# The dense tokens' second layers as three products of hi and lo parts, with nine row buffers in place of twelve

## The chip, the cores and the metric

The kernel runs on one core of a Trainium2 chip. The metric is the device time of one execution in microseconds; less is better. Rows of the profile name the engines: PE is TensorE (PEld its weight loads), DVE VectorE, ACT ScalarE, POOL GpSimd and SP SyncE.

## The reference, cut to what matters

Two transformer blocks run one after the other. The last layer of the second is a retrieval of single-neuron experts (`peer_ffn`), for 512 tokens of width 1024 with 16,384 experts. Each token has eight heads with 16 chosen experts each:

```python
idx = jnp.take_along_axis(cand_i, top_pos, axis=-1)
gate = jax.nn.softmax(top_s.astype(jnp.float32), axis=-1).astype(h.dtype)
...
act = jax.nn.gelu(jnp.einsum('thkd,td->thk', expert_u[ib], hb), approximate=False)
return jnp.einsum('thk,thkd->td', gb * act, expert_v[ib])
```

The first layer is a dot product of a token with a row of `expert_u`, then a GELU and the gate; the second layer is the weighted sum of rows of `expert_v`. The result is added to `x` and normalized. All of it is float32.

## The kernel before

The retrieval (`phase_d`) treats its 512 tokens in two ways. The first 256 (NS = 2 blocks of 128) are gathered: for every token and choice one row of `peer_u_rows` is fetched by an indirect DMA from GpSimd (128 rows of 4 KB each, 0.524 MB a gather, 128 gathers a block), and VectorE makes the dot product (L1355). Later the rows of `peer_v` are fetched the same way, and TensorE sums them: four gathers make a group, and a group is multiplied in one burst of eight float32 matmuls with a 32-column weight (L1384). The other 256 tokens (ND) are dense: all 16,384 experts are computed for them in NJ = 128 steps of 128 experts, and the gate, which is zero nearly everywhere, is multiplied in.

The last stage of the kernel is the loop over these 128 steps. A step has a weight `w` of 128 experts by 256 tokens (in SBUF as `ge` for the first 68 steps, and loaded back as `gl` and multiplied with the gate, loaded as `g`, on VectorE for the last 60, in groups of four steps: L1474, L1476, L1481), and a half of `vp`, a load of 128 x 2 x 1024 float32 (1 MB) of `peer_v` made once in two steps on SP's queue from a ring of four buffers. It multiplies them in four matmuls of 128x128 by 512 (L1495), two for each block of 128 tokens. The profile shows each of these float32 matmuls as two records.

The same loop advances two generators. `gathered_u` yields once for each gathered `peer_u` row and is pulled once a step in the first 60 steps, as long as rows are left; 50 of the 256 are. `gathered_v` is pulled every second step: it fetches the four gathers of the group two ahead, and then issues the burst of the group that is due. Both take their buffers from `gather`, which holds a list `rp` of two pools, `sb` with six row buffers and `lp` with six, and takes them strictly in turn. TensorE's instructions of the loop keep the order of the program; those of the other engines are ordered by the framework's scheduler when the kernel is built. Each engine then works in that fixed order, and waits for semaphores.

`x` is the dense tokens' input to the first layer, in `sb`, [128, 8, 256]; it has no reader once the first layers are done. Elsewhere in the kernel hi and lo parts are used already: `split` (L59, L60) makes a hi part with a ScalarE copy into a float32r tile, and a lo part by a VectorE subtraction, and `mm3` (L71) makes three products of them.

Of the kernel before, what the change touches and what calls it, by code (L numbers as in the profile page):

```python
# [11 lines left out]
FT = mybir.dt.float32  # L12
FR = mybir.dt.float32r
# [5 lines left out]
AF = mybir.ActivationFunctionType  # L19
OP = mybir.AluOpType  # L20
# [3 lines left out]
D = 1024  # L24
# [1091 lines left out]
def phase_d(k):  # L1116
    tc, nc, I = k.tc, k.nc, k.I
    gain = lambda n, c: k.vecs[:, VOFF[n] + c:VOFF[n] + c + 1]
    tt, ts, stt = nc.vector.tensor_tensor, nc.vector.tensor_scalar, nc.vector.scalar_tensor_tensor
    act = nc.scalar.activation  # L1120
    hx = k.hT[:, :, NM:]

    NJ, JG, TB, ND, NS = 128, 4, 32, 256, 2
# [7 lines left out]
    with ExitStack() as ctx:  # L1131
        dr = ctx.enter_context(tc.tile_pool(name="d_dram", bufs=1, space=bass.MemoryType.DRAM))
        sb = ctx.enter_context(tc.tile_pool(name="d_sb", bufs=1, reuse_waits="tile"))
# [21 lines left out]
        x = sb.tile([128, 8, ND], FT, name="x")  # L1155
        ht = [sb.tile([128, D], FT, name=f"ht{j}") for j in range(NS)]
        for s in range(2):
            o = slice(N0 * s, N0 + ND * s)
            for c in range(8):
                y = x[:, c] if s else xs[c // 4][:, c % 4]  # L1160
# [171 lines left out]
        out, rp = {}, []  # L1332

        def residual(po, j):

            hr = lp.tile([128, 8, 128], FT, name="hr", bufs=1)
            nc.scalar.dma_start(hr, hdr[:, :, 128 * j:128 * j + 128])
            for c in range(8):
                nc.tensor.matmul(po[c // 4][:, 128 * (c % 4):128 * (c % 4) + 128], hr[:, c], k.ident,
                                 start=False, stop=False, skip_group_check=True)  # L1340
# [56 lines left out]
        def pull(g, n):  # L1397
            for _ in range(n):
                if next(g, 0) == 0:
                    return False  # L1400
            return True
# [29 lines left out]
        for n in range(JR + JP):  # L1431
# [4 lines left out]
            else:  # L1436
                i = (n - JR) % JG
# [13 lines left out]

        lp = ctx.enter_context(tc.tile_pool(name="d_lp", bufs=2, reuse_waits="tile"))
        ps = ctx.enter_context(tc.tile_pool(name="d_po", bufs=1, reuse_waits="tile", space=PS))
        rp.append((lp, 6))
        for j in range(NS, 4):
            out[j] = [ps.tile([128, 512], FT, name=f"o{j}{i}") for i in range(2)]
        z = lp.tile([128, 4096], FT, name="z", bufs=1)
# [7 lines left out]
        def ahead(i):  # L1465

            if i >= NJ or ns[i] < JR:
                return
            n, j = ns[i], ns[i] % JG
            if j == 0:  # L1470
                g = lp.tile([128, NG, JG, TB], FT, name="g4", bufs=2)
                w = lp.tile([128, JG, ND], FT, name="gl", bufs=2)
                gl[n // JG] = w, g
                nc.scalar.dma_start(g, gdr[:, :, n - JR:n - JR + JG].rearrange("b p j t -> p b j t"))  # L1474
                if n < JR + JP:
                    nc.scalar.dma_start(w, st[:, n - JR:n - JR + JG])  # L1476
            w, g = gl[n // JG]
            if n >= JR + JP:
                u_chunk(n, w[:, j])
            b = w[:, j].rearrange("p (b t) -> p b t", t=TB)  # L1480
            tt(b, b, g[:, :, j], op=OP.mult)  # L1481
# [3 lines left out]
        with tc.manual_schedule(engines={mybir.EngineType.PE}):  # L1485
            for i in range(AH):
                ahead(i)
            for i, n in enumerate(ns):
                ahead(i + AH)
                if i % 2 == 0:  # L1490
                    vp = k.load(I["peer_v"].rearrange("(a j) d -> a j d", j=NJ)[:, n:n + 2], [128, 2, 1024])
                w = gl[n // JG][0][:, n % JG] if n >= JR else ge[n // JA][:, n % JA]
                for t in range(ND // 128):
                    for c in range(2):
                        nc.tensor.matmul(out[NS + t][c], w[:, 128 * t:128 * t + 128],  # L1495
                                         vp[:, i % 2, 512 * c:512 * c + 512],
                                         start=i == 0, stop=i == NJ - 1, skip_group_check=True)
                    if i == 0:
                        residual(out[NS + t], NS + t)
                if i < NJ // 2 - 4:  # L1500
                    pull(ga, 1)
                if i % 2:
                    pull(rows_left, 1)
# [4 lines left out]
        for j in range(4):  # L1508
            y = sb.tile([128, D], FT, name="rows", bufs=6)
# [13 lines left out]
def body(ctx, tc, I, out):  # L1523
# [37 lines left out]
    phase_b(k)  # L1561
    phase_c(k)
    phase_d(k)


# [106 lines left out]
```

## Time and profile before

| | |
|---|---|
| median of 3 runs | 3019.58 us (3007.23 to 3020.39) |
| the profiled execution's own time | 3018.37 us |
| its span in the profile | 3016.6 us |
| TensorE busy in the span | 2713.6 us (90%) |
| VectorE, ScalarE, GpSimd busy | 1224.5, 623.2, 591.7 us |
| mean transfer rate over the span | 303 GB/s |

The loop that is changed runs from about 2389 us to the end. Busy time counts an engine's instructions, and the ends of matmuls are modelled, so a busy TensorE need not be at its peak. The DMA share is the mean busy share of the core's 16 DMA engines; packets that overlap can take it a little over 1. A gather is timed from its issue on GpSimd to the landing of its last byte.

### The profile page before, as it was taken

What the parts mean: (1) busy time and instruction counts of PE and PEld (TensorE: products, weight loads), DVE (VectorE), ACT (ScalarE), POOL (GpSimd) and SP (SyncE); (2) the same over time, 40 slices, a digit from 0 to 9 for tenths busy, and PEclk for the clock granted to TensorE, in tenths of its full rate; (3) what the DMA queues carried; (4) which work ended last, traced back from release to release, by engine and by line L of the source; (5) the groups of instructions that cost most, each with busy time, mean ns of one, the idle gap of its engine ahead of it and who ended that gap; (6) DMA issues with size and microseconds to landing.
All of it is one profiled execution on the core that took longest, in us unless ns stands there. A gap on an engine that the chain in (4) does not pass through costs nothing. (4 is left out here: it accounts for less than half of the span.)

```text
span 3016.6 us, 35266 instructions
## 1 busy us (share of the span) xinstructions
PE 2713.6 (90%) x13794; PEld 1594.1 (53%) x13794; DVE 1224.5 (41%) x3040; ACT 623.2 (21%) x1304; POOL 591.7 (20%) x600
## 2 busy tenths in 40 slices
PE   8999888887888777699999997999998499999997
PEld 6877422322232222377777786888887333333332
DVE  5444411111111111268855389985888522200001
ACT  4333200000000000265333121122555300000000
POOL 1000100000000000000000005454433256544442
PEclk9979999999999999899999998999999699999999
DMA  4104899999999999912113239999999699999996
GB/s 158 42 1 154 367 421 421 421 421 421 420 421 420 421 421 376 376 60 85 56 56 112 92 132 355 365 381 361 379 363 350 225 399 412 412 410 363 401 401 252
DMA packets 185453, 912.93 MB, mean 303 GB/s; under 512 B 18864, under 2 KB 38464, under 8 KB 112192
## 3 DMA queue, kind: packets, MB, share of 16 engines
q1 hardware_dynamic: 83664, 602.85, 49.7%
q0 software_dynamic: 73728, 268.47, 23.0%
q10 hardware_dynamic: 27888, 39.29, 3.6%
q8 instruction: 110, 1.80, 0.2%
q14 instruction: 63, 0.52, 0.0%
HBM read 890.61 MB, written 19.92 MB: 302 GB/s over the span
## 5 line engine op out<-in xcount | busy, mean ns | idle before, releaser
L1328 PE MATMUL pa<-x,w 128*128 128x256 f32 x2048 | 455.4, 381 | 0.0
L1328 PEld LDWEIGHTS pa<-x,w 128*128 128x128 f32 x2048 | 385.9, 191 | 50.6
L1355 DVE SCALAR_TENSOR_TENSOR rows<-rows,ht 128x1024 f32<-128x1024 f32 x256 | 310.5, 1218 | 237.5 <-DMA rows<-in_peer_u_rows,ia 211.4
L1346 POOL DMA_INDIRECT rows<-in_peer_u_rows,ia x256 | 287.8, 1124 | 440.1 <-DVE rows L1355 211.1
L1346 POOL DMA_INDIRECT rows<-in_peer_v,iat x256 | 253.0, 988 | 292.1 <-PE os L1384 151.1
L712 PE MATMUL pr<-w,xs 128*32 128x512 f32 x1024 | 212.4, 697 | 91.6 <-DMA w<-in_expert_up 91.4
L732 PE MATMUL px<-w,ht 128*32 128x512 f32 x1024 | 223.2, 599 | 44.9 <-DMA w<-in_expert_down 35.5
L1495 PE MATMUL o<-w,ge 128*128 128x512 f32 x544 | 243.4, 600 | 0.0
L1495 PE MATMUL o<-w,gl 128*128 128x512 f32 x480 | 215.5, 602 | 4.4 <-DVE gl L1481 4.4
L71 PE MATMUL pm<-xg,w8h 128*128 128x512 f32 x640 | 206.4, 402 | 3.5 <-ACT cc L942 1.4
L712 PE MATMUL pg<-w,xs 128*32 128x512 f32 x1024 | 178.7, 612 | 19.3 <-DMA w<-in_expert_gate 19.3
L960 POOL MEMSET acc<- 128x1024 f32 x1 | 1.0, 952 | 936.4 <-PE px L732 936.4
L712 PEld LDWEIGHTS pr<-w,xs 128*32 128x32 f32 x1024 | 46.0, 124 | 245.1 <-DMA w<-in_expert_up 168.7
L1495 PEld LDWEIGHTS o<-w,ge 128*128 128x128 f32 x544 | 100.8, 191 | 139.4 <-issue 139.4
L732 PEld LDWEIGHTS px<-w,ht 128*32 128x32 f32 x1024 | 53.4, 109 | 203.0 <-DMA w<-in_expert_down 95.8
L718 DVE SCALAR_TENSOR_TENSOR hd<-pr,ga,hd 128x512 f32<-128x512 f32 x16 | 12.0, 751 | 361.6 <-PE pr L712 361.6
L1495 PEld LDWEIGHTS o<-w,gl 128*128 128x128 f32 x480 | 89.4, 191 | 131.0 <-issue 122.9
L1384 PE MATMUL os<-rows,z 128*32 128x512 f32 x1024 | 144.6, 600 | 5.4 <-DMA rows<-in_peer_v,iat 4.3
L1481 DVE TENSOR_TENSOR gl<-gl,g 128x256 f32<-128x256 f32 x60 | 21.5, 420 | 305.2 <-DMA gl<-st 305.2
L71 PEld LDWEIGHTS pm<-xg,w8h 128*128 128x128 f32 x640 | 120.8, 190 | 33.7 <-ACT w8h L59 2.0
L745 DVE TENSOR_TENSOR hT<-hT,po 128x512 f32<-128x512 f32 x128 | 86.0, 687 | 128.7 <-PE po L744 127.3
L59 ACT ACTIVATE w8h<-w 128x1024 fp32r<-128x1024 f32 (+3 forms) x101 | 90.8, 901 | 218.7 <-PE pm L71 106.3
(561 smaller groups left out, 3601.8 us busy)
## 6 DMA issues: line engine op xcount, KB each, us to landing
w<-in_expert_up SPq DMA_DIRECT2D x128, 1024.0 KB, 19.8
w<-in_expert_gate SPq DMA_DIRECT2D x128, 1024.0 KB, 19.8
w<-in_expert_down SPq DMA_DIRECT2D x128, 1024.0 KB, 19.8
w<-in_peer_u SPq DMA_DIRECT2D x64, 1024.0 KB, 8.1
w<-in_peer_v SPq DMA_DIRECT2D x64, 1024.0 KB, 8.3
w<-in_peer_wq SPq DMA_DIRECT2D x16, 1024.0 KB, 4.8
w<-in_w_out SPq DMA_DIRECT2D x8, 1024.0 KB, 4.8
st<-kept ACTq DMA_DIRECT2D x15, 512.0 KB, 9.3
```

The lines of the kernel that those rows point to most:

```text
L59: nc.scalar.activation(hi, src, AF.Copy)
L71: nc.tensor.matmul(o, w[:, c, :], x[:, c, s], start=first and c == 0 and n == 0, stop=last and c == kc - 1 and n == 2)
L712: nc.tensor.matmul(p[s], xs[:, 4 * half + c, s], ws[e][:, c], start=half == 0 and c == 0, stop=half == 1 and c == 3, skip_group_check=True)
L718: stt(hd, pu, ga[:, 1:2], hd, op0=OP.mult, op1=OP.mult)
L732: nc.tensor.matmul(pd[n][s], ht[:, 2 * half + f, s], ws[e][:, f, 512 * n:512 * n + 512], start=half == 0 and f == 0, stop=half == 1 and f ...
L745: tt(hx[:, c], hx[:, c], p, op=OP.add)
L1328: nc.tensor.matmul(p[:, :ND], w[:, c], x[:, c], start=c == 0, stop=c == 7)
L1346: nc.gpsimd.indirect_dma_start(out=r, out_offset=None, in_=rows, in_offset=bass.IndirectOffsetOnAxis(ap=idx, axis=0))
L1355: stt(r, r, 1.0, ht[j], op0=OP.mult, op1=OP.mult, accum_out=dots[:, n:n + 1])
L1384: nc.tensor.matmul(po[i][32 * g:32 * g + 32], z[:, o:o + 32], rs[g][:, 512 * i:512 * i + 512], start=r == 0, stop=r == 31, skip_group_chec ...
L1481: tt(b, b, g[:, :, j], op=OP.mult)
L1495: nc.tensor.matmul(out[NS + t][c], w[:, 128 * t:128 * t + 128], vp[:, i % 2, 512 * c:512 * c + 512], start=i == 0, stop=i == NJ - 1, skip_ ...
```

## The change

The dense tokens' second layer, one float32 matmul for each pair of operands, becomes three matmuls of float32r parts: hi by hi, hi by lo, and lo by hi. For that, each step makes hi and lo parts of the weight (`wp`, two buffers) and of the half of `vp` (`vs` in `lp` for even steps, and the tile `x` in `sb` for odd ones, one buffer each), by copies on ScalarE (`act`) and subtractions on VectorE (`tt`). The room comes from the row buffers of `lp`, which are three now and not six; `sb` keeps six.

```diff
-        rp.append((lp, 6))
+        rp.append((lp, 3))
...
                 w = gl[n // JG][0][:, n % JG] if n >= JR else ge[n // JA][:, n % JA]
+
+                wp = lp.tile([128, 2, ND], FR, name="wp", bufs=2)
+                vs = (sb if i % 2 else lp).tile([128, 2, D], FR, name="x" if i % 2 else "vs", bufs=1)
+                for y, z2 in ((w, wp), (vp[:, i % 2], vs)):
+                    act(z2[:, 0], y, AF.Copy)
+                    tt(z2[:, 1], y, z2[:, 0].bitcast(FT), op=OP.subtract)
                 for t in range(ND // 128):
-                    for c in range(2):
-                        nc.tensor.matmul(out[NS + t][c], w[:, 128 * t:128 * t + 128],
-                                         vp[:, i % 2, 512 * c:512 * c + 512],
-                                         start=i == 0, stop=i == NJ - 1, skip_group_check=True)
+                    for m, (hw, hv) in enumerate(((0, 0), (0, 1), (1, 0))):
+                        for c in range(2):
+                            nc.tensor.matmul(out[NS + t][c], wp[:, hw, 128 * t:128 * t + 128],
+                                             vs[:, hv, 512 * c:512 * c + 512], start=i == 0 and m == 0,
+                                             stop=i == NJ - 1 and m == 2, skip_group_check=True)
```

## Rows read from the trace of the kernel before

**Rows 1.** The page: busy time, share of the span and instructions by engine.
```profile
PE 2713.6 (90%) x13794; PEld 1594.1 (53%) x13794; DVE 1224.5 (41%) x3040; ACT 623.2 (21%) x1304; POOL 591.7 (20%) x600
```

**Rows 2.** Windows of the last stage: busy by engine, clock, DMA share, GB/s.
```profile
core 0: us, PE busy (x) PEld busy (x) DVE busy (x) ACT busy (x) POOL busy (x), PEclk, DMA share, GB/s
...
2440.00:2665.00 225.00, 220.96 (x718) 77.90 (x716) 53.35 (x87) 0.31 (x1) 134.40 (x133) 1.00 1.02 412
...
2732.00:2980.00 248.00, 248.00 (x888) 94.14 (x888) 17.21 (x48) 0.00 (x0) 105.91 (x112) 1.00 1.02 396
```

**Rows 3.** TensorE's timeline, first part: start, us, group [idle before]; first, middle, last.
```profile
2405.74 1.92 PE L1384 MATMUL os<-rows,z 128*32 128x512 f32 x16 [0.55 <-ACT z L1378]
...
2564.21 7.13 PE L1495 MATMUL o<-w,ge 128*128 128x512 f32 x16
2571.28 1.06 PE L1384 MATMUL os<-rows,z 128*32 128x512 f32 x6
2572.54 1.90 PE L1384 MATMUL os<-rows,z 128*32 128x512 f32 x10 [0.20 <-DMA rows<-in_peer_v,iat]
2574.37 7.13 PE L1495 MATMUL o<-w,ge 128*128 128x512 f32 x16
...
2674.20 1.92 PE L1384 MATMUL os<-rows,z 128*32 128x512 f32 x16
```

**Rows 4.** TensorE's timeline, second part.
```profile
2855.08 1.92 PE L1384 MATMUL os<-rows,z 128*32 128x512 f32 x16
2856.93 7.13 PE L1495 MATMUL o<-w,gl 128*128 128x512 f32 x16
2864.00 1.92 PE L1384 MATMUL os<-rows,z 128*32 128x512 f32 x16
```

**Rows 5.** VectorE's timeline, second part.
```profile
2829.38 1.43 DVE L1481 TENSOR_TENSOR gl<-gl,g 128x256 f32<-128x256 f32 x4 [17.06 <-DMA gl<-st]
2847.93 1.43 DVE L1481 TENSOR_TENSOR gl<-gl,g 128x256 f32<-128x256 f32 x4 [17.12 <-DMA gl<-st]
```

**Rows 6.** TensorE's timeline in an earlier stage that uses hi and lo parts.
```profile
1449.24 0.63 PE L71 MATMUL pm<-xg,w8h 128*128 128x512 f32 x2
...
1451.35 0.63 PE L71 MATMUL pm<-xg,w8h 128*128 128x512 f32 x2
```

**Rows 7.** Groups by line and shape: the splits; busy us, mean ns, idle before.
```profile
L59 ACT ACTIVATE w8h<-w 128x1024 fp32r<-128x1024 f32 x71 | 74.9, 1056 | 140.1 <-PE pm L71 52.7 <-PE uu L71 23.4 <-issue 17.8
...
L59 ACT ACTIVATE w8h<-w 128x256 fp32r<-128x256 f32 x8 | 3.3, 412 | 9.5 <-PE uu L71 4.8 <-PE mm L71 4.7
...
L60 DVE TENSOR_TENSOR w8l<-w,w8h 128x1024 fp32r<-128x1024 f32 x71 | 87.6, 1235 | 35.6 <-ACT w8h L59 34.9
...
L60 DVE TENSOR_TENSOR w8l<-w,w8h 128x256 fp32r<-128x256 f32 x8 | 3.4, 419 | 1.5 <-ACT w8h L59 1.5
```

**Rows 8.** GpSimd's timeline, second part.
```profile
2848.34 1.17 POOL L1346 DMA_INDIRECT rows<-in_peer_v,iat  x1 [4.25 <-PE os L1384]
2849.81 0.94 POOL L1346 DMA_INDIRECT rows<-in_peer_v,iat  x1 [0.30 <-issue]
2851.06 0.94 POOL L1346 DMA_INDIRECT rows<-in_peer_v,iat  x1 [0.30 <-issue]
```

**Rows 9.** GpSimd's timeline, first part.
```profile
2564.37 1.37 POOL L1346 DMA_INDIRECT rows<-in_peer_v,iat  x1 [0.34 <-PE os L1384]
...
2570.70 0.94 POOL L1346 DMA_INDIRECT rows<-in_peer_v,iat  x1 [1.28 <-DMA rows<-in_peer_v,iat]
...
2574.54 1.37 POOL L1346 DMA_INDIRECT rows<-in_peer_v,iat  x1 [0.34 <-PE os L1384]
```

**Rows 10.** Landing of gathers, windows 1800:1900, 2450:2650, 2700:2727, 2760:2950 in order.
```profile
DMA to landing us min/median/max: 5.1/6.5/9.8
...
DMA to landing us min/median/max: 11.1/12.4/14.9
...
DMA to landing us min/median/max: 5.2/6.5/6.7
...
DMA to landing us min/median/max: 6.8/8.8/13.7
```

**Rows 11.** The DMA view, 2389 to 3006 us.
```profile
DMA packets 71131, 235.11 MB, mean 381 GB/s; under 512 B 6228, under 2 KB 23508, under 8 KB 63425
```

## The prediction, made before the changed kernel ran

> **What bounds the kernel now.** I read the page first for the total [rows 1], then the windows of the last stage, then the timelines of TensorE, GpSimd and VectorE there, then the landing times of its transfers. Only the loop of 128 steps is changed; I count it in pairs of steps, since one pair takes one load of dense rows and one group of four gathered `peer_v` rows. A pair is 16 records of dense products (eight plain float32 matmuls, two records each) and then one burst of 16 records of L1384.
>
> TensorE looks like the bound: it is busy 221 of 225 us and 248 of 248 us in the two long windows [rows 2]. The same rows say that the DMA engines are just as full: share 1.02, at 412 and 396 GB/s. Which of the two sets the pace is read from the period of a pair.
>
> In the first part, while gathered `peer_u` rows are also fetched, dense runs start at 2564.21 and 2574.37, a period of 10.16 us, and L1384 stops after six records until a gathered row lands [rows 3]. A pair moves 1.05 MB of dense rows, 4 x 0.524 MB of `peer_v` rows and 2 x 0.524 MB of `peer_u` rows, 4.19 MB. Over 412 GB/s that is 10.17 us. So the transfers set this part. From the first burst to 2674.20 there are 27 periods in 268.5 us [rows 3], 9.94 us in the mean, so some early ones, while the queues filled, were shorter.
>
> In the second part a pair takes 2864.00 - 2855.08 = 8.92 us with no wait shown [rows 4], which is TensorE's own 7.07 + 1.85 us. But VectorE's products for `gl`, four steps at a time, come at 2829.38 and 2847.93, so every 18.55 us, or 9.27 us a pair [rows 5]. They wait for the loads of `gl`. A pair here moves 1.05 + 2.10 + 0.52 = 3.67 MB, which at the 396 GB/s of this window is 9.27 us too. TensorE runs at 8.92 us only because it eats up a reserve of buffers that were loaded ahead. This part is within 4% of the transfers' pace, on the wrong side.
>
> **The change part by part.** *The products.* Per pair, 16 records in 7.07 us become 24 matmuls of the hi/lo kind. Such triples run elsewhere in this kernel: from 1449.24 to 1451.35 are three triples, 2.11 us, 0.235 us a matmul [rows 6]. 24 x 0.235 = 5.63 us. A pair of TensorE work falls from 8.92 to 7.48 us, and 64 x 1.44 = 92 us of TensorE work go away. By the part above nearly none of it is on the path: the 27 pairs with `peer_u` are at the transfers' pace, the 30 pairs with `gl` already ask for more than the transfers give, and about seven pairs between them move 3.15 MB, 7.64 us at 412 GB/s. At most 7 x 1.3 = 9 us can come out there.
>
> *The splits.* A step adds two copies on ScalarE, 0.41 and 1.06 us, and two subtractions on VectorE, 0.42 and 1.24 us [rows 7]. Over 128 steps that is 188 us of ScalarE and 212 us of VectorE. A pair adds 3.32 us to VectorE, which is busy 53 of 225 us in the first part and 17 of 248 us in the second [rows 2], so neither engine fills. Two buffers of `vs`/`x` alternate, so the split of a step may start when the step two before it has ended; a step (2.82 us) and a burst (1.85 us) of TensorE cover 1.06 + 1.24 us plus the small pair, with 1.5 us to spare. I cost it at nothing while that cover holds. It is gone where a subtraction queues on VectorE behind a wait for a gathered `peer_u` row or for `gl`: then TensorE waits as long as that transfer is late. That is a rival below.
>
> *Gathers under VectorE's work.* A gather that was issued under the four `gl` products took 1.17 us, the next, issued almost when they were done, 0.94 us [rows 5, 8]. VectorE will be busy about a third of a pair more. One gather in the chain of a pair, delayed 0.23 us one time in three: 64 x 0.08 = 5 us; bounds nothing and 64 x 3 x 0.23 = 44 us. The Trainium skill ("SBUF — State Buffer", Who interferes with whom) holds that a tensor_tensor doesn't hold up the writing of such descriptors, which would make this term zero; the row is a quarter longer.
>
> *The row buffers.* This is the term that decides. `gather` takes the two pools in strict turn. With six and six, a gather reuses the buffer of the twelfth gather before it. With six and three, every second gather needs the sixth before it. With `peer_u` a pair makes six gathers (two `peer_u`, four `peer_v`), and the lp pool gets three of them: exactly one pair. So the second `peer_v` gather of a pair must wait until the burst of the pair before has released a buffer, and the third and fourth stand behind it in GpSimd's queue. Today the group is released two pairs ahead: a burst's end at 2572.54 + 1.90 = 2574.44 lets the gather at 2574.54 go, for the burst two periods later [rows 3, 9].
>
> The new loop of a pair is: burst ends, 0.1 us to the release, three gathers issued with the last starting 2.5 us after the first (starts are 1.25 us apart at the least [rows 8]), its landing L after its start, then the ten records of the burst that need it, 1.9 us [rows 3], with about 0.2 us of semaphores. Period = L + 4.7 us. That the order is so strict is read from today's queue, where a pair's four `peer_v` gathers start between 2564.37 and 2570.70 with nothing of another pair between them [rows 9]. L is 12.4 us in the saturated first part, 6.5 us where `peer_u` alone is gathered [rows 10]. Fewer gathers in flight means a shorter L, so I take 7.0 us, near the low row: 11.7 us. Bounds: if the scheduler puts gathers of the other pool ahead of the waiting one the loop is L + 2.2 us and the transfers' 10.17 us stays; with L 8.8 us it is 13.5 us. Sum for the 27 pairs: 27 x 11.7 = 316 against 268, **+48 us** (bounds +6 and +96).
>
> Without `peer_u`, the lp pool gets two gathers of a pair and has three buffers, so only the fourth gather waits for the burst just before: period = L + 2.2 us. In the seven pairs before `gl` is loaded L is 6.5 us [rows 10]: 8.7 us, 7 x -0.2 = **-1 us**. In the 30 pairs with `gl`, L is now 6.8 at the least and 8.8 in the median [rows 10], so 9.0 to 11.0 us. A longer period unloads the queues, so I take the low side, but not under the transfers' 9.27: 9.5 us. 30 x (9.5 - 8.92) = **+17 us** (bounds +2 and +62).
>
> Sum: +48 - 1 + 17 + 5 = +69 us on the profiled execution's 3018.4 us, 3087 us. That execution is 1.2 us under the median of the runs shown, which I leave out.
>
> **The rivals.** *No change: the gathers are not late.* If the latency of a gather falls far enough once fewer are under way, or other gathers are put ahead of the waiting one, the shorter depth costs nothing and the transfers set both parts as now: +6 us in the first part, +10 us for the `gl` pairs at 9.27 us, up to 9 us back between them, so 3010 to 3034, about 3020 us. Against it stand landing times that never fall under 5.1 us in any of the four windows [rows 10]. The Trainium skill ("DMA: Bandwidth & Descriptors", Anatomy of one DMA) gives 2.0 us plus the bytes over 436 GB/s for one transfer, an estimate of 3.2 us for a gather; by that both loops would be hidden, and the trace's 6.5 to 12.4 us disagree with it.
>
> *Faster.* One mechanism only: with TensorE no longer near the pace, buffers are given back sooner wherever the queues are not yet full, and the transfers reach 412 GB/s throughout. From 2389 to 3006 us 235.11 MB moved [rows 11], which at 412 GB/s is 571 us in place of 617: 46 us less, 2972 us at best, and more likely 2985 to 3003. It decides if the lp loop stays under 9 us in every pair, that is if L stays under 6.8 us in the second part. The medians of 8.8 and 12.4 us speak against it. That TensorE's whole 92 us come off (2926 us) I rule out, since 235.11 MB would have to move at 448 GB/s.
>
> *Much slower: subtractions behind waits.* VectorE takes its work in order. Its `gl` products wait about 17 us for their load every four steps [rows 5]. Nothing stands behind them today; afterwards subtractions do. If the order puts them two or three steps early, TensorE has about two steps and a burst, 7.5 us, of work left against a load that takes longer, and each of 15 groups loses 3 to 7 us, the same again for `peer_u` rows in the first part. With the terms above: 3140 to 3260 us, about 3190.
>
> **How the numbers follow.** The forecast (the lp pool's loop, 3040 to 3140) has 0.60, no change 0.18, faster 0.09, much slower 0.13. A measurement of this kernel tells about 0.5%, 15 us, from no change. So faster 0.09, same 0.18, slower 0.73. The time given is the likeliest case's, 3087. The range leaves out faster and the upper half of much slower: 3008 to 3190.
>
> **What would show it.** If right: TensorE's share in the last stage falls well under 0.98, L1384's bursts break in two at a wait for a `peer_v` row in nearly every pair, GpSimd's waits name L1384 before a gather that lands just before the next burst, the DMA share in the first part falls under 1.0, and the pair's period there is 11 to 13 us. The new matmuls stand 0.235 us apart. The prediction is wrong if the period of the first part stays at 10.2 us and that of the second goes under 9 us (no change or faster), or if the dense products wait for VectorE's subtractions rather than L1384 for rows (much slower).

## The result, and the profile after

The changed kernel takes 3081.2 us in the median of 4 runs (3078.7 to 3082.6), against 3014.8 us for the kernel before in 4 runs; ratio 1.0216, 95% interval 1.0201 to 1.0232. It is slower by about 2.2%, 66 us. The profiled execution took 3080.5 us, 62 us more than that of before; its span is 3078.7 us.

The page gives the totals by engine (busy us, share of the span, instructions), and two of its groups:

```profile
PE 2696.0 (88%) x14306; PEld 1697.8 (55%) x14306; DVE 1431.4 (46%) x3296; ACT 797.6 (26%) x1560; POOL 597.1 (19%) x600
...
L1384 PE MATMUL os<-rows,z 128*32 128x512 f32 x1024 | 217.1, 648 | 86.6 <-DMA rows<-in_peer_v,iat 83.2
...
L1502 PE MATMUL o<-vs,wp 128*128 128x512 f32 x768 | 198.2, 407 | 5.6 <-ACT vs L1497 5.5
```

VectorE and ScalarE carry the splits: 207 and 174 us more than in [rows 1]. TensorE has less work and sits idle 86.6 us before L1384, waiting for gathered `peer_v` rows. Before the new dense products (L1502) it sits idle 5.6 us. So the products are hardly ever late; the bursts of gathered rows are.

Two windows of the last stage, in the columns of [rows 2]; the second is the stretch of [rows 2], the first starts at 2406 and not at 2440 us:

```profile
2406.00:2665.00 259.00, 222.35 (x918) 117.29 (x919) 124.39 (x175) 60.20 (x89) 137.56 (x133) 0.95 0.95 360
2732.00:2980.00 248.00, 218.08 (x1021) 128.69 (x1020) 95.88 (x140) 70.17 (x105) 97.58 (x101) 0.97 0.96 358
```

The DMA engines, at a share of 1.02 and 412 and 396 GB/s in [rows 2], now stand at 0.95 and 0.96 and move about 360 GB/s. TensorE fell from 100% to 88% in the second. TensorE and the transfers, both full before, have slack: what sets the pace now is a latency.

TensorE's timeline in the first part shows it; 26 of the 27 bursts after the first have such a wait:

```profile
2584.82 2.88 PE L1502 MATMUL o<-x,wp 128*128 128x512 f32 x12
2587.63 1.04 PE L1384 MATMUL os<-rows,z 128*32 128x512 f32 x2
2589.20 1.05 PE L1384 MATMUL os<-rows,z 128*32 128x512 f32 x4 [0.53 <-DMA rows<-in_peer_v,iat]
2590.50 1.90 PE L1384 MATMUL os<-rows,z 128*32 128x512 f32 x10 [0.24 <-DMA rows<-in_peer_v,iat]
2592.33 3.02 PE L1502 MATMUL o<-vs,wp 128*128 128x512 f32 x12
2595.19 2.88 PE L1502 MATMUL o<-x,wp 128*128 128x512 f32 x12
2598.00 1.04 PE L1384 MATMUL os<-rows,z 128*32 128x512 f32 x2
2600.86 1.05 PE L1384 MATMUL os<-rows,z 128*32 128x512 f32 x4 [1.81 <-DMA rows<-in_peer_v,iat]
2602.14 1.90 PE L1384 MATMUL os<-rows,z 128*32 128x512 f32 x10 [0.23 <-DMA rows<-in_peer_v,iat]
```

Two dense steps now take 5.67 us (2592.33 to 2598.00), without a gap. The burst, whole or in two pieces in [rows 3], breaks in three, and from its first record to the next dense step takes 4.7 us in the first of these pairs (2587.63 to 2592.33) and 6 in the second, where 1.85 would do.

In the second part, where [rows 4] show no wait at all, 20 of 29 bursts break in two at the fourth gathered row, here in a period of 9.66 us:

```profile
2855.12 3.00 PE L1502 MATMUL o<-vs,wp 128*128 128x512 f32 x12
2857.96 2.88 PE L1502 MATMUL o<-x,wp 128*128 128x512 f32 x12
2860.77 1.06 PE L1384 MATMUL os<-rows,z 128*32 128x512 f32 x6
2862.95 1.90 PE L1384 MATMUL os<-rows,z 128*32 128x512 f32 x10 [1.12 <-DMA rows<-in_peer_v,iat]
2864.78 3.02 PE L1502 MATMUL o<-vs,wp 128*128 128x512 f32 x12
```

GpSimd's and VectorE's timelines of that stretch of the first part say why the rows are late:

```profile
2586.46 0.94 POOL L1346 DMA_INDIRECT rows<-in_peer_u_rows,ia  x1 [0.30 <-issue]
2589.34 0.94 POOL L1346 DMA_INDIRECT rows<-in_peer_v,iat  x1 [1.95 <-DVE rows L1355]
2591.83 0.94 POOL L1346 DMA_INDIRECT rows<-in_peer_u_rows,ia  x1 [1.55 <-PE os L1384]
2593.07 0.94 POOL L1346 DMA_INDIRECT rows<-in_peer_v,iat  x1 [0.30 <-issue]
2594.32 0.94 POOL L1346 DMA_INDIRECT rows<-in_peer_v,iat  x1 [0.30 <-issue]
2595.56 0.94 POOL L1346 DMA_INDIRECT rows<-in_peer_v,iat  x1 [0.30 <-issue]
...
2602.14 0.94 POOL L1346 DMA_INDIRECT rows<-in_peer_v,iat  x1 [4.39 <-DVE rows L1355]
```

```profile
2586.42 1.30 DVE L1498 TENSOR_TENSOR vs<-w,vs 128x1024 fp32r<-128x1024 f32 x1 [0.53 <-issue]
2587.84 1.23 DVE L1355 SCALAR_TENSOR_TENSOR rows<-rows,ht 128x1024 f32<-128x1024 f32 x1
...
2599.50 1.23 DVE L1498 TENSOR_TENSOR x<-w,x 128x1024 fp32r<-128x1024 f32 x1 [0.52 <-ACT x L1497]
2600.64 1.22 DVE L1355 SCALAR_TENSOR_TENSOR rows<-rows,ht 128x1024 f32<-128x1024 f32 x1
```

As the burst ends, at 2590.50 + 1.90 = 2592.40 us, a `peer_u` gather that waited for L1384 and three `peer_v` gathers go out one behind the other. The next burst goes on at 2600.86 and at 2602.14, 6.54 and 6.58 us after the second and the third of them: by these times each burst waits for gathers that went out as the burst before it ended. One `peer_v` gather of the pair goes ahead of them (2589.34, and 2602.14 in the next pair), and it waits for a buffer that VectorE's dot product gives back. That dot product stands behind a subtraction of the new splits. At 2587.84 this cost little: its row was gathered at 2581.48, and at the same 6.5 us it landed at about 2588.0 (an estimate). At 2600.64 it cost some 2 us: that row was gathered at 2591.83, and by the same estimate was there at 2598.4.

The loop can be split by the starts of the records of L1384: 64 bursts, and in each the time from its first record to its last. Worked out in this way from the two traces (us):

| | before | after | difference |
|---|---|---|---|
| first burst starts at | 2405.7 | 2406.2 | +0.4 |
| first 27 periods | 268.5 | 309.3 | +40.8 |
| next 7 periods | 64.9 | 64.8 | -0.1 |
| last 29 periods | 264.7 | 285.6 | +20.9 |
| of these 63 periods, inside bursts | 109.7 | 257.1 | +147 |
| of these 63 periods, the rest (dense steps) | 488.4 | 402.6 | -86 |

The dense steps became 86 us shorter, near the 92 us of TensorE's work that the new products take away, and the bursts became 147 us longer.

### The profile page after: what moved, and what is told of

Same layout as the page of the kernel before. It is cut to its first block, busy times and chain, and to the rows that moved or that the text cites. A ratio compares the mean times of both kernels' runs of the same rounds, so it can differ in the third digit from the quotient of the medians.

```text
span 3078.7 us, 36929 instructions
## 1 busy us (share of the span) xinstructions
PE 2696.0 (88%) x14306; PEld 1697.8 (55%) x14306; DVE 1431.4 (46%) x3296; ACT 797.6 (26%) x1560; POOL 597.1 (19%) x600
## 5 line engine op out<-in xcount | busy, mean ns | idle before, releaser
L1384 PE MATMUL os<-rows,z 128*32 128x512 f32 x1024 | 217.1, 648 | 86.6 <-DMA rows<-in_peer_v,iat 83.2
L1502 PE MATMUL o<-vs,wp 128*128 128x512 f32 x768 | 198.2, 407 | 5.6 <-ACT vs L1497 5.5
L1502 PEld LDWEIGHTS o<-vs,wp 128*128 128x128 f32 x768 | 142.0, 192 | 93.4 <-issue 50.0
L1502 PE MATMUL o<-x,wp 128*128 128x512 f32 x768 | 184.5, 389 | 0.0
L1384 PEld LDWEIGHTS os<-rows,z 128*32 128x32 f32 x1024 | 39.4, 111 | 220.7 <-DMA rows<-in_peer_v,iat 154.7
L1502 PEld LDWEIGHTS o<-x,wp 128*128 128x128 f32 x768 | 144.1, 188 | 29.9
L740 DVE SCALAR_TENSOR_TENSOR yl<-px,ga,yh 128x512 fp32r<-128x512 f32 x32 | 24.0, 750 | 266.9 <-ACT yh L739 265.2
```

The costliest lines, as they stand in the source:

```text
L740: stt(yl[:, o], pd[n], ga[:, 0:1], yh[:, o].bitcast(FT), op0=OP.mult, op1=OP.subtract)
L1384: nc.tensor.matmul(po[i][32 * g:32 * g + 32], z[:, o:o + 32], rs[g][:, 512 * i:512 * i + 512], start=r == 0, stop=r == 31, skip_group_chec ...
L1502: nc.tensor.matmul(out[NS + t][c], wp[:, hw, 128 * t:128 * t + 128], vs[:, hv, 512 * c:512 * c + 512], start=i == 0 and m == 0, stop=i == ...
```

## The experiments

Each kernel was timed beside the kernel before on the same chip. All were profiled. "Strict turn" is the order of `gather` in the changed kernel (sb, lp, sb, lp).

| kernel | products | row buffers | median us | ratio (95% interval) |
|---|---|---|---|---|
| the changed one | hi, lo | 6 + 3, strict turn | 3081.2 | 1.0216 (1.0201 to 1.0232) |
| f32_nine_turn | float32 | 6 + 3, strict turn | 3065.9 | 1.0170 (1.0148 to 1.0193) |
| f32_turn_splits | float32, splits unread | 6 + 3, strict turn | 3076.7 | 1.0208 (1.0183 to 1.0234) |
| one_product_turn | hi by hi only | 6 + 3, strict turn | 3117.1 | 1.0313 (1.0277 to 1.0349) |
| f32_nine_two_one | float32 | 6 + 3, two to one | 3031.1 | 1.0043 (1.0025 to 1.0062) |
| hilo_two_one | hi, lo | 6 + 3, two to one | 3037.3 | 1.0073 (1.0053 to 1.0093) |
| hilo_gl_three | hi, lo | 6 + 3, two to one, third `gl` | 3017.7 | 1.0000 (0.9985 to 1.0016) |
| hilo_ten | hi, lo | 6 + 4, three to two | 3010.6 | 0.9980 (0.9963 to 0.9998) |
| hilo_ten_late | hi, lo | 6 + 4, three to two | 3007.6 | 0.9974 (0.9958 to 0.9990) |
| f32_hr_two | float32 | 6 + 6 | 3013.3 | 0.9988 (0.9976 to 1.0000) |
| f32_half_loads | float32, half the dense loads | 6 + 6 | 2989.0 | 0.9918 (0.9897 to 0.9939) |
| hilo_ten_half_loads | hi, lo, half the dense loads | 6 + 4, three to two | 2950.6 | 0.9799 (0.9776 to 0.9822) |
| hilo_turn_half_loads | hi, lo, half the dense loads | 6 + 3, strict turn | 3070.9 | 1.0191 (1.0170 to 1.0212) |

**The buffers alone** (f32_nine_turn), an edit of the kernel before:

```diff
-        rp.append((lp, 6))
+        rp.append((lp, 3))
```

> The kernel before, plain float32, with only the lp pool cut from six row buffers to three; no splits, no new products. Theory (the lp pool's turn decides): the loop of a pair is the landing of a gather plus 4.7 us in the first part and plus 2.2 us in the second, with no regard to the products, so the whole loss of the change or nearly all of it is here: 3060 to 3085 us, and L1384 waits for rows inside its bursts. Rival (splits on VectorE and ScalarE are what costs): 3010 to 3025 us, as before.

Measured 1.0170, 47 us by the medians: some three quarters of the loss, with neither splits nor new products. Its trace has the waits inside the bursts, for example in the first part:

```profile
2561.03 7.13 PE L1495 MATMUL o<-w,ge 128*128 128x512 f32 x16
2568.09 1.90 PE L1384 MATMUL os<-rows,z 128*32 128x512 f32 x6
2571.51 1.90 PE L1384 MATMUL os<-rows,z 128*32 128x512 f32 x10 [1.51 <-DMA rows<-in_peer_v,iat]
2573.34 7.13 PE L1495 MATMUL o<-w,ge 128*128 128x512 f32 x16
```

In this kernel the landings of gathers can be read too (the trace of the changed one pairs none), from 2420 to 2680 and from 2760 to 2980 us:

```profile
DMA to landing us min/median/max: 4.9/6.5/10.6
...
DMA to landing us min/median/max: 5.9/7.3/10.0
```

The first was 12.4 us in [rows 10]: with fewer under way a gather lands in half the time, and the loop is slower all the same, because it has to wait for each.

**The turn** (f32_nine_two_one and hilo_two_one). Nine buffers as in the change, but sb is drawn twice for each draw of lp, so that each gather needs the ninth before it. From the changed kernel (and the same for float32):

```diff
-        rp.append((lp, 3))
+        rp[:] = [(sb, 6), (lp, 3), (sb, 6)]
```

> The kernel before in plain float32 with nine row buffers, two gathers to sb for each one to lp. Theory (the turn): the depth is nine for every gather, the first part stays at the transfers' 10.2 us or a little over, the second at 8.92 us: 3012 to 3035 us. Rival (the number of buffers in whatever order): 3050 us or more.

> The changed kernel, still nine row buffers, but two gathers are given to the sb pool for each one given to lp, so that every gather needs the ninth before it and not, for every second one, the sixth. Theory (the turn): in the first part only the last gather of a pair still waits for the burst just before (landing plus 2.2 us, near the transfers' 10.2 us), in the second part none does: 3010 to 3035 us. Rival (splits): no change, 3070 to 3090 us. Rival (the number of buffers, in whatever order): 3050 to 3075 us.

Measured 1.0043 and 1.0073. One line that only changes the order in which the two pools are drawn gives back 35 us in float32 and 44 us with the new products. The second came out 2 us above its expected range; most of what was left is in the first part, where 27 periods take 287.1 us against 268.5 in the kernel before. In the second part the trace of hilo_two_one has waits of the dense products for VectorE (18 us there), which the changed kernel hardly has:

```profile
2836.94 0.73 PE L1502 MATMUL o<-vs,wp 128*128 128x512 f32 x2
2842.04 4.63 PE L1502 MATMUL o<-vs,wp 128*128 128x512 f32 x10 [4.37 <-DVE vs L1498]
```

**The splits by themselves** (f32_turn_splits). To f32_nine_turn, whose products stay plain float32 on `w` and `vp`, the splits are added with nothing that reads them:

```diff
+                wp = lp.tile([128, 2, ND], FR, name="wp", bufs=2)
+                vs = (sb if i % 2 else lp).tile([128, 2, D], FR, name="x" if i % 2 else "vs", bufs=1)
+                for y, z2 in ((w, wp), (vp[:, i % 2], vs)):
+                    act(z2[:, 0], y, AF.Copy)
+                    tt(z2[:, 1], y, z2[:, 0].bitcast(FT), op=OP.subtract)
```

> The float32 kernel with three lp buffers in strict turn (it took 3066 us), and the splits are made as well, but nothing reads them: the products stay plain float32. Shows what the splits cost by themselves, through GpSimd's gathers and the queues, without TensorE waiting for them. Theory (the splits' own work costs little, some 5 us): 3062 to 3078 us. Rival (their work on VectorE and ScalarE is what makes the changed kernel 15 us slower than this one without them): 3078 to 3095 us.

Measured 1.0208, 11 us over the kernel without them, within the range of the first theory but at its upper end; the two intervals just overlap. The two profiles are 17 us apart: 5 us are in the loop (+7.2, +0.7 and -3.0 us in the three stretches of the table above), and 12.4 us are a later start of the loop than in f32_nine_turn. Where the loop starts differed by up to 16 us between kernels of the same work, and these runs don't say why in each case.

**TensorE's work** (one_product_turn). The changed kernel with hi by hi alone; hi by lo and lo by hi are left out (and `stop` is set at the product that is left):

```diff
-                    for m, (hw, hv) in enumerate(((0, 0), (0, 1), (1, 0))):
+                    for m, (hw, hv) in enumerate(((0, 0),)):
```

> The changed kernel with the hi by hi product alone: the two products with a lo part are left out, the splits are still made. Takes 16 matmuls of 0.235 us, 3.8 us, of TensorE's work from a pair, 240 us in all. Theory (TensorE is off the path): 3060 to 3085 us. Rival (TensorE's work still sets part of the pace): 2840 to 2950 us.

Measured 1.0313, 3117 us: with 240 us of TensorE's work taken out, the kernel is 36 us slower than the changed one. That TensorE's amount of work doesn't set the pace holds, but the number was missed, and the reason is in the windows of its loop and in its timeline:

```profile
2406.00:2744.00 338.00, 211.32 (x648) 68.86 (x648) 138.32 (x202) 69.04 (x107) 171.05 (x156) 0.77 0.90 325
...
2577.88 1.05 PE L1384 MATMUL os<-rows,z 128*32 128x512 f32 x2
2581.35 1.05 PE L1384 MATMUL os<-rows,z 128*32 128x512 f32 x4 [2.42 <-DMA rows<-in_peer_v,iat]
2584.70 3.62 PE L1384 MATMUL os<-rows,z 128*32 128x512 f32 x10 [2.30 <-DMA rows<-in_peer_v,iat]
```

The granted clock (the column before the DMA share) is 0.77, against 0.95 in the changed kernel, and the ten records of a burst that take 1.90 us above take 3.62 us. These ten records lie in the loop of the lp pool, between the landing of a row and the release of its buffer. Over the 27 bursts after the first they take 40 us more than 1.90 each, against 8 us in the changed kernel; the 27 periods are 31 us longer (340.3 against 309.3 us), and most of the 36 us is there.

**More depth** (hilo_ten). Ten buffers fit if `hr` takes its room from a buffer of `g`:

```diff
-            hr = lp.tile([128, 8, 128], FT, name="hr", bufs=1)
+            hr = lp.tile([128, 8, 128], FT, name="hr", tag="g4", bufs=2)
...
-        rp.append((lp, 3))
+        rp[:] = [(sb, 6), (lp, 4), (sb, 6), (lp, 4), (sb, 6)]
```

> The changed kernel with ten row buffers, six in sb and four in lp, given out three to two, so that each gather needs the tenth before it; hr takes its room from a buffer of g. Theory (depth of the row buffers): in the first part no gather of a pair waits for the burst just before, so the part loses its last excess and stays at the transfers' pace; against the two-to-one kernel with nine buffers (3037 us) 5 to 20 us less: 3017 to 3032 us. Rival (what is left of the loss comes from subtractions behind gl on VectorE): 3032 to 3040 us, with dense products still waiting for VectorE in the second part.

Measured 0.9980. From the changed kernel 71 us have come back, more than expected, all of the loss. The loop's first 27 periods take 270.2 us, as in the kernel before (268.5), and in the second part TensorE has its free pace of 7.56 us a pair, until a load of `gl` is due:

```profile
2775.09 0.73 PE L1502 MATMUL o<-vs,wp 128*128 128x512 f32 x2
2787.46 4.64 PE L1502 MATMUL o<-vs,wp 128*128 128x512 f32 x10 [11.64 <-DVE vs L1498]
2791.89 3.26 PE L1502 MATMUL o<-x,wp 128*128 128x512 f32 x12
2795.08 1.92 PE L1384 MATMUL os<-rows,z 128*32 128x512 f32 x16
...
2802.64 1.93 PE L1384 MATMUL os<-rows,z 128*32 128x512 f32 x16
2804.50 3.06 PE L1502 MATMUL o<-vs,wp 128*128 128x512 f32 x12
2807.39 2.88 PE L1502 MATMUL o<-x,wp 128*128 128x512 f32 x12
2810.20 1.92 PE L1384 MATMUL os<-rows,z 128*32 128x512 f32 x16
```

VectorE's timeline beside it:

```profile
2784.50 0.76 DVE L1481 TENSOR_TENSOR gl<-gl,g 128x256 f32<-128x256 f32 x2 [16.10 <-DMA gl<-st]
2785.18 0.42 DVE L1498 TENSOR_TENSOR wp<-gl,wp 128x256 fp32r<-128x256 f32 x1
2785.51 0.75 DVE L1481 TENSOR_TENSOR gl<-gl,g 128x256 f32<-128x256 f32 x2
2786.19 1.22 DVE L1498 TENSOR_TENSOR vs<-w,vs 128x1024 fp32r<-128x1024 f32 x1
```

The subtractions stand behind a product that waits for its load: the wait that the prediction had as a rival. What TensorE gains in the pairs between goes into these stops, 29 us of waits for VectorE in all; the last 29 periods take 271.0 us together, 9.34 us each, against 264.7 us in the kernel before.

**The subtractions behind `gl`** (hilo_gl_three, hilo_ten_late). The first is hilo_two_one with the `hr` edit and a third buffer for `gl`; the second is hilo_ten with the product of `gl` moved from three steps ahead to its own step:

```diff
-                w = lp.tile([128, JG, ND], FT, name="gl", bufs=2)
+                w = lp.tile([128, JG, ND], FT, name="gl", bufs=3)
```

> The changed kernel with nine row buffers two to one, and three gl buffers in place of two, so that a gl load may start one group (about 18 us) earlier. Theory (subtractions stand behind gl products that wait for a load): the waits of the dense products for VectorE in the second part, some 40 us in the two-to-one kernel, shrink, and the time falls from 3037 to 3010 to 3025 us. Rival (the transfers set the second part): the waits go elsewhere, to L1384 or to the loads, and the time stays within 6 us of 3037 us.

```diff
-            b = w[:, j].rearrange("p (b t) -> p b t", t=TB)
-            tt(b, b, g[:, :, j], op=OP.mult)
...
+        def gated(n):
+            if n < JR:
+                return ge[n // JA][:, n % JA]
+            w, g = gl[n // JG]
+            b = w[:, n % JG].rearrange("p (b t) -> p b t", t=TB)
+            tt(b, b, g[:, :, n % JG], op=OP.mult)
+            return w[:, n % JG]
...
-                w = gl[n // JG][0][:, n % JG] if n >= JR else ge[n // JA][:, n % JA]
+                w = gated(n)
```

> The kernel with ten row buffers, and the gl product of a step is emitted in its own step, right before its split, where it was emitted three steps ahead; its loads stay three steps ahead. Theory (order on VectorE): fewer subtractions stand behind a product that waits for its load, and 5 to 20 us go against the ten-buffer kernel. Rival (the scheduler places the products by its own clock anyway, or the transfers set the pace): within 6 us of the ten-buffer kernel.

The third buffer gave 20 us by the medians, as the theory said; the two profiled executions are only 9.5 us apart. In both the loop starts at about 2402 us; the last 29 periods fall from 267.9 to 257.6 us, under the 264.7 us of the kernel before, and the waits of the dense products for VectorE from 20.2 to 12.6 us, where the theory had counted some 40. Moving the product gave 3 us, within the noise, as its rival said.

**Whose lead is it?** hilo_ten is 0.2% under the kernel before. The `hr` edit comes with it, and its loop starts at 2394.6 us, 11 us earlier; from there to the end both take 611 to 612 us. So the `hr` edit was made alone on the kernel before (f32_hr_two; the diff of `hr` above):

> The kernel before, plain float32 with twelve row buffers, and one edit of the ten-buffer kernel alone: hr takes its room from the two buffers of g, so its two first loads need not wait for each other. Theory (the ten-buffer kernel's lead of 0.2% comes from this earlier start of the loop, 2394.6 against 2405.7 us, and not from the products): 3003 to 3012 us, as the ten-buffer kernel. Rival (the lead comes from TensorE's saved work): 3013 to 3020 us, as before.

Measured 3013.3 us, 0.9988 (0.9976 to 1.0000), at the lower edge of the rival's range, 1 us over the theory's. Its loop does start at 2395.4 us, but the first 27 periods then take 274.7 us, 6 us more. It can't be told from hilo_ten or from the kernel before. At this level it stays open whether the new products give anything; it is not more than 0.2 to 0.3%.

**Under the transfers.** The three half-load kernels load the dense `peer_v` rows once in four steps and use each load twice, which leaves out half of the dense rows, 0.52 MB of a pair:

```diff
-                if i % 2 == 0:
+                if i % 4 == 0:
```

> The kernel before (plain float32, twelve buffers) with a load of dense peer_v rows once in four steps in place of two, each used twice: half of the dense rows are left out, 0.52 MB of a pair. Theory (transfers set the first part, TensorE's 8.92 us a pair is the next bound): the first part falls from 10.2 to about 9.0 us a pair, the second stays at 8.92: 2980 to 3000 us. Rival (TensorE sets the pace everywhere): 3010 to 3020 us.

> The ten-buffer kernel with hi and lo products and the same half of the dense loads left out. Theory (TensorE's 92 us were hidden under the transfers): now they show in part, a pair falls to the transfers' 8.9 us in the first part and 7.9 us in the second: 2935 to 2975 us, well under the float32 kernel with the same loads. Rival (the splits and the subtractions behind waits eat the saving whatever the transfers do): 2980 to 3005 us.

> The changed kernel (three lp buffers in strict turn) with the same half of the dense loads left out. Theory (the loop of the lp pool is a latency, not a rate): it is shortened only as far as a gather lands sooner, by 0.5 to 1 us a pair: 3020 to 3055 us. Rival (the changed kernel is bound by the rate of transfers): 52 to 81 us less than 3081 us, 3000 to 3029 us.

Measured 2989.0, 2950.6 and 3070.9 us. The second is 38 us under the first. Of that 17 us are the earlier start of its loop (2391.9 against 2409.0 us); in the 63 periods the new products are worth 24.4 us (+5.3, -7.2 and -22.6 us in the three stretches). With all the bytes the same comparison, hilo_ten against the kernel before, gives +0.9 us. The kernel in strict turn gains only 10 us from an eighth to a seventh fewer bytes in a pair; even the theory had expected 26 to 61 us, so its number was missed. In the profiles its first 27 periods are 7.6 us shorter than in the changed kernel and its last 29 4.7 us longer; from 2732 to 2980 us the DMA share is 0.86 and the granted clock 0.92, against 0.96 and 0.97. So it isn't bound by the rate of transfers; how much of the missing gain the clock took wasn't measured.

## Why the prediction was right, point by point

*What bounds the kernel.* Right. Transfers set the first part at 10.16 us a pair, and TensorE's time lay under them: with enough row buffers (hilo_ten) the first part stays at 10.2 us a pair in the median, with the DMA engines at 1.02 and 412 GB/s from 2440 to 2665 us as in [rows 2], although its TensorE work is 1.4 us shorter; and with half of the dense loads a part of the saving comes out.

*The products.* The pace of 0.235 us was right (5.67 us for 24), and so was that nearly none of it would show. 86 us went out of the dense steps and into the bursts.

*The row buffers.* The mechanism was right: the lp pool's strict turn. Its size was partly right by luck. First part: +48 us expected, +40.8 measured, but of that the buffers alone make +25.4 (293.9 us for 27 periods in f32_nine_turn, 10.89 us each against 11.7 forecast). Two terms of the loop were off, in opposite ways, and this is the luck. L was 6.5 us and not 7.0. And the order was not the one assumed: the scheduler put one `peer_v` gather ahead, where it waited for a dot product of VectorE, and a `peer_u` gather before the other three. So the last of the three starts 3.16 us after the burst's end (2592.40 to 2595.56) and not 2.6. With 6.58 us of landing and the ten records, 1.90, that pair takes 11.64 us; the 27 periods of the changed kernel took 11.46 in the mean. The forecast's 0.2 us of semaphores stands in no row. Second part: +17 expected, +20.9 measured, and the buffers alone make +19.9. L of 7.3 us in f32_nine_turn plus 2.2 is 9.5 us; the 29 periods took 9.85, and 9.13 in the kernel before. The forecast's 8.92 was the pace of a smooth stretch, so both its ends were low, and their difference came out.

*The seven pairs between.* -1 us expected, -0.1 measured.

*The splits and the gathers under VectorE's work.* 5 us expected in all. Measured by medians: the splits 11 us, and the products on top of them 4 us, which the intervals don't tell from nothing. This term was too small, and one for TensorE's clock was missing. In the first part of the profiles it is +7 us for the splits and +8 us more when the products read them. For the 7 us a part of the road is seen: a subtraction stands ahead of a dot product on VectorE, and a gather waits for the buffer that the dot product gives back. Gathers issued under VectorE's work are seen too, of 1.36 us at 2570.84 (under a dot product) and 1.68 us at 2577.53 (under a subtraction) where 0.94 is usual. How the 7 us divide between the two wasn't measured. By the Trainium skill's rule on the port ("SBUF — State Buffer", Who interferes with whom) a tensor_tensor, as the subtraction is one, holds up GpSimd's reads but not the writing of descriptors (the latter is marked there as inferred). This trace doesn't agree, unless the issue of an indirect gather counts as a read, which no run here shows: of 59 gathers of the loop issued mostly under a subtraction of 128x1024, 24 took over 1.05 us, up to 1.99; the 100 issued with VectorE idle all took 0.95 us or less.

For the 8 us the trace shows another road, which the forecast doesn't have:

```profile
2492.83 1.05 PE L1384 MATMUL os<-rows,z 128*32 128x512 f32 x2
2495.15 1.05 PE L1384 MATMUL os<-rows,z 128*32 128x512 f32 x4 [1.27 <-DMA rows<-in_peer_v,iat]
2497.70 3.62 PE L1384 MATMUL os<-rows,z 128*32 128x512 f32 x10 [1.50 <-DMA rows<-in_peer_v,iat]
```

The ten records take 3.62 us and not 1.90, in a window of the lower clock (0.83 from 2490 to 2510 us). Five of these 27 bursts are so, 8 us in all, and none in f32_turn_splits. No run changes the clock alone, so that this is the cause is read from the trace and not tested.

*The rivals.* "No change" fell with f32_nine_turn. The estimate of 3.2 us for a gather that stood beside it, from the Trainium skill ("DMA: Bandwidth & Descriptors", Anatomy of one DMA), is half of the shortest median measured in the loop, 6.5 us. "Faster" failed on the loop, as its condition said: L would have had to stay under 6.8 us in the second part, and in f32_nine_turn it is 7.3. "Much slower", the subtractions behind waits, was not what the changed kernel ran into: 5.6 us before L1502. Its mechanism is real, and came up as soon as the row buffers no longer set the pace: 11.64 us in a single stop of hilo_ten.

*The sum.* 3087 us forecast, 3081.2 measured; the sum for the profiled execution was +69 us, its measured difference 62 us.

## What to carry to other kernels

Before a saving on a busy engine is booked, the transfers' rate in the same window is to be set against the bytes of a period: two resources can be full at once, and the saving shows only down to the second. Two pools drawn in strict turn have the depth of twice the smaller one, not of the sum: with 6 + 3 buffers every second gather waits for the sixth before it, and drawing them two to one gave back 35 of 47 us in float32 and 44 of 66 us with the new products, with no byte more. A latency that grew under a full queue (12.4 us) shrinks when less is under way (6.5 us), but a loop that waits for it each time pays it in full. The Trainium skill ("Perfetto Trace Analysis", Optimization Strategy) reads the same gap, repeated on an engine that should be full, as something that can mean too little room for buffers; the bursts of the changed kernel agree with it, 83.2 us of idle in all.

## What was not expected of the hardware

Less work on TensorE made the kernel slower. With a third of the products the granted clock fell to 0.77 and 0.82 in the two halves of the loop, and a part of each burst ran at the lower of the two clock levels, 1.2 GHz: ten records in 3.62 us and not 1.90. Before these ten records TensorE had done some 2 us of dense work and two records of the burst, waited for rows about 2 us, done four records and waited about 2 us again. The changed kernel itself is at 0.95 and 0.97 in the loop, where the kernel before is at 1.00.
